# Banded attention of a trunk kernel: context scores as two fp32r passes of split operands, and both mask products at an item's end

## The chip, the cores and the metric

One core of one Trainium2 chip runs the whole step in one launch. The metric is the device time of a run in microseconds. The kernel before was run three times: 2095.13, 2097.68 and 2099.02 us, median 2097.68. All times of engines and instructions come from one further, profiled execution.

## The reference

One inference step of a backbone of two layers (width 1024) for 128 context tokens and 256 latent tokens that share all weights. Each layer is a half-step SwiGLU, a mixer stage and another half-step SwiGLU. The mixer stage projects the tokens with one matrix `w_in` into the columns of four branches (A long convolution, B differential attention, C windowed attention, D retention) and their gates, and adds their gated outputs up. The change lies in branch C, which has 8 query heads in 2 key heads of 64, and, for latent tokens, a band of keys plus all context keys in one softmax with a learned sink:

```python
    s_band = jnp.einsum('bnqhgd,bnkhd->bnhgqk', qb, kb).astype(jnp.float32) * scale
    s_band = jnp.where(valid[None, :, None, None], s_band, NEG_INF)
    s_ctx = jnp.einsum('bnqhgd,bchd->bnhgqc', qb, k_ctx).astype(jnp.float32) * scale
    s_sink = jnp.broadcast_to(sink.astype(jnp.float32).reshape(WIN_KV_HEADS, WIN_GROUP)[None, None, :, :, None, None],
...
    p = jax.nn.softmax(jnp.concatenate([s_band, s_ctx, s_sink], axis=-1), axis=-1)
```

Context tokens attend to the 128 context keys alone, in `window_dense_block`, with the same scale and sink. `NEG_INF` stands at band positions farther than 128 tokens.

## The kernel before, in words

All large products are made of two fp32r halves of each operand: a value is split into a high part and the rest (`split`, line 456: a copy on ScalarE, L412, rounds to the high part, a subtraction on VectorE, L389, makes the low part), and `mm3` (L383) adds high by high, low by high and high by low. The tokens stand as 384 columns, so most matmuls of TensorE (`mm`, L376) are 128x384: some 10,800 of them, called the main stream here, go through the weights in a fixed order. `run_plan` (L461) loads each weight block raw by a DMA of SyncE's queue, `splits` makes its halves wh and wl in four slots ahead of their use, and every half has some 24 main matmuls in these stages.

The branches' own work is written as generators (`diff_side`, `hy_side`, `win_side`, `ret_side`), and `pump` (L602) fits their steps between the main matmuls. It goes by modelled clocks of the engines: every helper (`mm`, `act`, `tt`) adds a modelled cost, and a step is taken when the modelled VectorE and ScalarE are not too far behind TensorE, when two PSUM banks are free, and when its inputs are due. A step taken writes its instructions into each engine's queue there; every engine then works its queue in order. New work, or more or fewer free tiles, therefore shifts where later steps land. Tiles come from three sets: L (30 of 512 columns), M (26 of 384 columns, and L if none is free), and B, the 8 PSUM banks, each handed out longest-free first.

`win_side` (L1525) does branch C of one layer. It normalises the queries, transposes them by `feat_mm` (four banks, one for each pair of heads, 128 context and 256 latent columns), and brings them into SBUF: the latent columns are split, in two halves of 64 partitions (one for each head), so that high and low part of a head stand above each other on 128 partitions (`qT`); the 128 context columns are copied plainly to `qc`, in fp32. Then the keys: reciprocal roots, norm, rotation, transposes, the latent keys split into `kh` and `kl`, the context keys copied plainly to `kc`.

Then 12 items (pair of heads `pr` 0 to 3, query tile `qt` 0 to 2; `qt` 0 is the context tile) go through `softmax_pipe` (L1382), which in its step i does `s3` of item i−4 (the product with the values), `s2` of i−3 (transposes), `s1` of i (scores), `s1c` of i−2 and `s1b` of i−1 (maximum, exponential, sums). `s1` fills two banks, one for each head c of the pair. A context item has one fp32 product of 64 partitions for each bank, which the trace shows as two records. A latent item has two fp32r products of 128 partitions and 384 columns (the stacked queries against `kh` and `kl`), then a product of the identity `identb` with the mask `maskb`, both bf16, 128x128, added to it. `s3` of a pair's last tile splits the pair's output from its bank into two M tiles, which frees that bank, and in the same step `s1` of the next pair but one's context item takes banks. When the branch is done, its output waits for the branch's weights in the main stream.

Of the kernel before, what the change touches and what calls it, by code (L numbers as in the profile page):

```python
# [11 lines left out]
F32R = mybir.dt.float32r  # L12
# [300 lines left out]
class Kern:  # L313
# [1211 lines left out]
    def win_side(self, l):  # L1525
        L, M, B, nc, S = self.L, self.M, self.B, self.nc, self.S
        while "wq" not in S:
            yield "w"
        ck, cv = L.get(), M.get()
# [5 lines left out]
        for t in range(3):  # L1535
            self.qk_norm(qs[t], 8, rs[:, 8 * t:8 * t + 8], t, self.sm(l, "gwq"), tl, 0)
            yield 0.0 if t < 2 else list(qs)
        qT, qc = [], L.get()
        for h in range(4):
            b = self.feat_mm(qs, 128 * h)  # L1540
            d = L.get(F32R)
            for c in range(2):
                r, o, n = slice(64 * c, 64 * c + 64), slice(64 - 64 * c, 128 - 64 * c), slice(256 * c, 256 * c + 256)
                self.split(d[r, n], d[o, n], b[r, 128:384])
            self.act(qc[:, 128 * h:128 * h + 128], b[:, 0:128])
            B.put(b)
            qT.append(d)
            if h % 2:
                yield 0.0
# [3 lines left out]
        kv = S.pop("wkv")  # L1553
# [11 lines left out]
        nc.gpsimd.dma_start(self.O["o_wk"][l], kv[0][:, 0:128])  # L1565
        nc.gpsimd.dma_start(self.O["o_wv"][l], kv[0][:, 128:256])
        L.put(tl)
        kT, kc = [], M.get()
        for h in range(2):
            b = self.feat_mm(kd + [ck], 128 * h)  # L1570
            kh, kl = M.get(F32R), M.get(F32R)
            self.split(self.nv(kh[:, :T]), self.nv(kl[:, :T]), self.pv(b[:, 128:512]))
            self.act(kc[:, 128 * h:128 * h + 128], b[:, 0:128])
            B.put(b)
            kT.append((kh, kl))
        L.put(ck, *kd)
        V = [k[:, 128:256] for k in kv] + [cv[:, 0:128]]
        yield qT + [qc, kc] + [x for p in kT for x in p]
        items = [(pr, qt) for pr in range(4) for qt in range(3)]
        py = {}  # L1580
        out = []
# [1 line left out]
        def s1(pr, qt):  # L1583
            nk = 384 if qt else 128
            kv_ = pr // 2
            ps = []
            for c in range(2):
                b = B.get()
                r = slice(64 * c, 64 * c + 64)
                if qt == 0:  # L1590
                    self.mm(b[:, :128], qc[r, 128 * pr:128 * pr + 128], kc[r, 128 * kv_:128 * kv_ + 128], True, True)
                else:
                    o = 256 * c + 128 * (qt - 1)
                    for i in range(2):
                        self.mm(b[:, :nk], qT[pr][:, o:o + 128], self.mv(kT[kv_][i][:, :nk]), i == 0, False)
                    mo = 128 if qt == 1 else 0
                    self.mm(b[:, mo:mo + 128], self.identb, self.maskb[:, 128 * (qt - 1):128 * qt], False, True)
                ps.append(b)
            return ps, nk, pr

        def s1b(ps, nk, pr):
# [37 lines left out]
        def s3(pr, qt, at):  # L1639
# [9 lines left out]
            if qt == 2:  # L1649
# [4 lines left out]
                out.append((hi, lo))  # L1654

        yield from self.softmax_pipe(items, s1, s1b, s1c, s1d, s2, s3)
        M.put(cv, kc, *[x for p in kT for x in p])
        L.put(qc, *qT, *kv)
        self.br[2] = out

    def ret_prep(self, l):
# [450 lines left out]
```

## Time and profile before

| what | value |
|---|---|
| time of the runs (median of three) | 2097.68 us |
| profiled execution, its own time | 2092.43 us |
| span in the profile | 2090.7 us |
| mean granted clock of TensorE | 0.996 |
| TensorE busy | 2060.9 us (99%) |
| VectorE busy | 1476.3 us (71%) |
| ScalarE busy | 960.1 us (46%) |
| share of the chain that ended last | TensorE 78%, VectorE 12%, ScalarE 4% |

The profiled execution's own time is 1.7 us over its span. TensorE's records overlap: a 128x384 matmul is recorded with some 0.33 us, while one starts about every 0.16 us, so its cost in a row of matmuls is the distance of starts and not the recorded length. A number in square brackets behind a row is the engine's idle time before it and what ended it. Names of tiles stand without their numbers: wh and wl are weight halves, hh and hl activations, raw the loaded weights, B a PSUM bank, L and M tiles, sm small columns.

### The profile page before, as it was taken

The page shows a single profiled execution, that of the slowest core. Times are in us where ns is not written, and L with a number is a line of the kernel's source. Part 1 is how long each engine was busy: PE and PEld are TensorE (multiplying, and loading weights), DVE is VectorE, ACT ScalarE, POOL GpSimd, SP SyncE. Part 2 cuts the span into 40 slices and gives each one's busy share as a digit, 9 for nine tenths or more (in the row PEclk, how much of TensorE's full clock was granted, in tenths as well). Part 3 has the DMA queues.
Part 4 walks back from the last instruction along what each step waited for, and adds up shares of the span by engine and source line. Part 5 has one row for each costly group of instructions (what it writes and reads, how often), then busy time and mean ns, then how long its engine had stood idle before and what let it go on. Part 6 is the DMA issues. An engine that isn't in the chain of part 4 may idle for free.

```text
span 2090.7 us, 33262 instructions
## 1 busy us (share of the span) xinstructions
PE 2060.9 (99%) x12994; PEld 1958.0 (94%) x12994; DVE 1476.3 (71%) x3156; ACT 960.1 (46%) x1661; POOL 31.4 (2%) x62
## 2 busy tenths in 40 slices
PE   9999999999999999999999999999999999999999
PEld 7999988899988998999999999888999889899999
DVE  5789779578764788877578995686787656754443
ACT  4443446664455435334444333456535543443332
POOL 0000000000000000000000000000000000000000
PEclk9999999999999999999999999999999999999999
DMA  8658463323232536662366773632233223533432
GB/s 317 241 201 321 151 226 124 113 102 122 113 116 99 194 139 233 222 210 102 109 244 229 246 255 120 248 133 104 101 130 124 102 101 108 198 121 115 156 120 100
DMA packets 88206, 340.39 MB, mean 163 GB/s; under 512 B 10416, under 2 KB 12912, under 8 KB 64624
## 3 DMA queue, kind: packets, MB, share of 16 engines
q1 hardware_dynamic: 83952, 326.41, 44.1%
q0 software_dynamic: 3808, 11.71, 1.7%
q8 instruction: 102, 1.67, 0.3%
q14 instruction: 56, 0.46, 0.1%
q10 hardware_dynamic: 288, 0.14, 0.0%
HBM read 334.82 MB, written 3.41 MB: 162 GB/s over the span
## 4 chain that ended last, share of the span: by engine, by line
PE 78%; DVE 12%; ACT 4%; issue 3%; DMA 3%; SPq 0%; ACTq 0%; DVEq 0%
PE B L376 76%; DVE L L400 3%; DVE wl L389 3%; ACT wh L412 2%; DMA L<-in_ada 2%; PE B L418 2%; DVE M L389 1%; DVE L L389 1%; DVE M L400 1%; ACT L L412 1%; ACT M L412 1%; DVE x L400 1%; DMA raw<-in_w1a 0%; DMA L<-in_adap 0%; SPq L582 0%
## 5 line engine op out<-in xcount | busy, mean ns | idle before, releaser
L389 DVE TENSOR_TENSOR wl<-raw,wh 128x1024 fp32r<-128x1024 f32 (+1 forms) x500 | 563.3, 1138 | 294.2 <-ACT wh L412 290.9
L376 PE MATMUL B<-hh,wh 128*128 128x384 f32 x2176 | 719.7, 331 | 2.0 <-ACT hh L412 2.0
L376 PE MATMUL B<-hh,wl 128*128 128x384 f32 x2176 | 711.7, 327 | 4.0 <-DVE wl L389 4.0
L376 PE MATMUL B<-hl,wh 128*128 128x384 f32 x2176 | 711.3, 327 | 0.8 <-DVE hl L400 0.8
L412 ACT ACTIVATE wh<-raw 128x1024 fp32r<-128x1024 f32 (+1 forms) x500 | 483.1, 982 | 326.3 <-PE B L376 250.7
L376 PE MATMUL B<-M,wh 128*128 128x384 f32 x1816 | 456.8, 328 | 0.2 <-ACT M L412 0.2
L376 PEld LDWEIGHTS B<-hh,wh 128*128 128x128 f32 x2176 | 412.2, 189 | 16.1 <-issue 9.3
L376 PEld LDWEIGHTS B<-hh,wl 128*128 128x128 f32 x2176 | 412.3, 189 | 6.7 <-DVE wl L389 6.2
L376 PEld LDWEIGHTS B<-hl,wh 128*128 128x128 f32 x2176 | 412.3, 189 | 1.9 <-DVE hl L400 1.9
L376 PEld LDWEIGHTS B<-M,wh 128*128 128x128 f32 x1816 | 321.3, 189 | 3.9 <-issue 1.4
L376 PE MATMUL B<-M,wl 128*128 128x384 f32 x928 | 303.1, 327 | 0.0
L400 DVE SCALAR_TENSOR_TENSOR L<-L,L 128x512 f32<-128x512 f32 x320 | 202.7, 691 | 2.2 <-ACT L L412 1.7
L412 ACT ACTIVATE M<-B 128x384 f32<-128x384 f32 (+2 forms) x254 | 113.9, 465 | 162.7 <-PE B L376 125.1
L376 PEld LDWEIGHTS B<-M,wl 128*128 128x128 f32 x928 | 175.7, 189 | 0.6 <-DVE wl L389 0.2
L389 DVE TENSOR_TENSOR M<-M,M 128x384 f32<-128x384 f32 (+2 forms) x200 | 110.1, 556 | 82.8 <-ACT M L412 80.5
L412 ACT ACTIVATE M<-M 128x384 fp32r<-128x384 f32 (+2 forms) x108 | 53.2, 499 | 246.6 <-DVE M L389 228.6
L376 PE MATMUL B<-wh,hh 128*128 128x512 f32 (+1 forms) x336 | 124.5, 370 | 0.2 <-ACT hh L412 0.2
L376 PE MATMUL B<-wh,hl 128*128 128x512 f32 (+1 forms) x336 | 122.7, 365 | 0.6 <-DVE hl L400 0.6
L376 PE MATMUL B<-wl,hh 128*128 128x512 f32 (+1 forms) x336 | 122.5, 365 | 0.0
L412 ACT ACTIVATE L<-B 128x512 f32<-128x512 f32 (+7 forms) x186 | 88.0, 517 | 63.8 <-PE B L376 43.8
L389 DVE TENSOR_TENSOR M<-M,B 128x384 f32<-128x384 f32 x88 | 48.6, 552 | 61.3 <-ACT M L412 61.3
L400 DVE SCALAR_TENSOR_TENSOR x<-B,mod,x 128x128 f32<-128x128 f32 (+1 forms) x160 | 59.0, 414 | 25.0 <-PE B L376 24.3
(162 smaller groups left out, 1862.4 us busy)
## 6 DMA issues: line engine op xcount, KB each, us to landing
raw<-in_win SPq DMA_DIRECT2D x74, 1024.0 KB, 4.8
L<-in_ada SPq DMA_DIRECT2D x192, 256.0 KB, 5.8
raw<-in_w1b SPq DMA_DIRECT2D x44, 1024.0 KB, 4.8
raw<-in_w1a SPq DMA_DIRECT2D x41, 1024.0 KB, 4.9
L<-in_adap SPq DMA_DIRECT2D x96, 256.0 KB, 7.4
raw<-in_w2a SPq DMA_DIRECT2D x32, 704.0 KB, 4.1
raw<-in_w2b SPq DMA_DIRECT2D x32, 704.0 KB, 4.0
raw<-in_wbr SPq DMA_DIRECT2D x16, 1024.0 KB, 4.8
```

Source lines behind the costliest of these rows:

```text
L376: self.nc.tensor.matmul(out, lhsT, rhs, start=start, stop=stop, **kw)
L389: self.nc.vector.tensor_tensor(out, a, b, op=op)
L400: self.nc.vector.scalar_tensor_tensor(out, a, s, b, op0=op0, op1=op1, accum_out=accum_out)
L412: self.nc.scalar.activation(out, a, f, **kw)
L418: self.nc.tensor.transpose(out, a, self.ident)
```

## The change

In each layer the context queries are split too: for each pair of heads two splits of 64 partitions by 128 columns follow the two of the latent columns, alternating with them, and fill two L tiles of fp32r (`qc`, a list now) in place of one plain copy into one L tile. The context keys are split into one L tile (`kc`: high parts in columns 0 to 255, low parts behind) in place of a plain copy into an M tile. The scores of a context item become two fp32r products of 128 partitions for each bank, against the high and the low keys. In all items both banks are taken at the start of `s1`, and in latent items the two mask products come behind all four score products. What is computed is the same.

```diff
--- before.py
+++ after.py
@@ -1535,14 +1535,17 @@
         for t in range(3):
             self.qk_norm(qs[t], 8, rs[:, 8 * t:8 * t + 8], t, self.sm(l, "gwq"), tl, 0)
             yield 0.0 if t < 2 else list(qs)
-        qT, qc = [], L.get()
+        qT, qc = [], []
         for h in range(4):
             b = self.feat_mm(qs, 128 * h)
             d = L.get(F32R)
+            if h % 2 == 0:
+                qc.append(L.get(F32R))
             for c in range(2):
                 r, o, n = slice(64 * c, 64 * c + 64), slice(64 - 64 * c, 128 - 64 * c), slice(256 * c, 256 * c + 256)
                 self.split(d[r, n], d[o, n], b[r, 128:384])
-            self.act(qc[:, 128 * h:128 * h + 128], b[:, 0:128])
+                n = slice(256 * (h % 2) + 128 * c, 256 * (h % 2) + 128 * c + 128)
+                self.split(qc[-1][r, n], qc[-1][o, n], b[r, 0:128])
             B.put(b)
             qT.append(d)
             if h % 2:
@@ -1565,17 +1568,17 @@
         nc.gpsimd.dma_start(self.O["o_wk"][l], kv[0][:, 0:128])
         nc.gpsimd.dma_start(self.O["o_wv"][l], kv[0][:, 128:256])
         L.put(tl)
-        kT, kc = [], M.get()
+        kT, kc = [], L.get(F32R)
         for h in range(2):
             b = self.feat_mm(kd + [ck], 128 * h)
             kh, kl = M.get(F32R), M.get(F32R)
             self.split(self.nv(kh[:, :T]), self.nv(kl[:, :T]), self.pv(b[:, 128:512]))
-            self.act(kc[:, 128 * h:128 * h + 128], b[:, 0:128])
+            self.split(kc[:, 128 * h:128 * h + 128], kc[:, 256 + 128 * h:384 + 128 * h], b[:, 0:128])
             B.put(b)
             kT.append((kh, kl))
         L.put(ck, *kd)
         V = [k[:, 128:256] for k in kv] + [cv[:, 0:128]]
-        yield qT + [qc, kc] + [x for p in kT for x in p]
+        yield qT + qc + [kc] + [x for p in kT for x in p]
         items = [(pr, qt) for pr in range(4) for qt in range(3)]
         py = {}
         out = []
@@ -1583,19 +1586,19 @@
         def s1(pr, qt):
             nk = 384 if qt else 128
             kv_ = pr // 2
-            ps = []
-            for c in range(2):
-                b = B.get()
-                r = slice(64 * c, 64 * c + 64)
-                if qt == 0:
-                    self.mm(b[:, :128], qc[r, 128 * pr:128 * pr + 128], kc[r, 128 * kv_:128 * kv_ + 128], True, True)
-                else:
-                    o = 256 * c + 128 * (qt - 1)
-                    for i in range(2):
+            ps = [B.get(), B.get()]
+            for c, b in enumerate(ps):
+                for i in range(2):
+                    if qt == 0:
+                        o, k = 256 * (pr % 2) + 128 * c, 256 * i + 128 * kv_
+                        self.mm(b[:, :128], qc[pr // 2][:, o:o + 128], kc[:, k:k + 128], i == 0, i == 1)
+                    else:
+                        o = 256 * c + 128 * (qt - 1)
                         self.mm(b[:, :nk], qT[pr][:, o:o + 128], self.mv(kT[kv_][i][:, :nk]), i == 0, False)
-                    mo = 128 if qt == 1 else 0
+            if qt:
+                mo = 128 if qt == 1 else 0
+                for b in ps:
                     self.mm(b[:, mo:mo + 128], self.identb, self.maskb[:, 128 * (qt - 1):128 * qt], False, True)
-                ps.append(b)
             return ps, nk, pr
 
         def s1b(ps, nk, pr):
@@ -1654,8 +1657,8 @@
                 out.append((hi, lo))
 
         yield from self.softmax_pipe(items, s1, s1b, s1c, s1d, s2, s3)
-        M.put(cv, kc, *[x for p in kT for x in p])
-        L.put(qc, *qT, *kv)
+        M.put(cv, *[x for p in kT for x in p])
+        L.put(kc, *qc, *qT, *kv)
         self.br[2] = out
 
     def ret_prep(self, l):
```

The order of the instructions moves at three places that matter here. The first is ScalarE's queue at the query split of layer 0: B0 and B5 are the banks of the first two pairs of heads, L14 and L17 before (L0 and L17 now) their latent tiles `qT`, and L0 before (L14 now) the context tile `qc`. Before:

```order
L412 ACTIVATE L14_221_5347<-B0_180_5343 64x256 x2
L412 ACTIVATE L0_220_5342<-B0_180_5343 128x128
L412 ACTIVATE L17_222_5357<-B5_181_5353 64x256 x2
L412 ACTIVATE L0_220_5342<-B5_181_5353 128x128
L412 ACTIVATE L19_223_5373<-B1_182_5369 64x256 x2
```

Now:

```order
L412 ACTIVATE L0_220_5346<-B0_180_5342 64x256
L412 ACTIVATE L14_221_5347<-B0_180_5342 64x128
L412 ACTIVATE L0_220_5346<-B0_180_5342 64x256
L412 ACTIVATE L14_221_5347<-B0_180_5342 64x128
L412 ACTIVATE L17_222_5360<-B5_181_5356 64x256
L412 ACTIVATE L14_221_5347<-B5_181_5356 64x128
L412 ACTIVATE L17_222_5360<-B5_181_5356 64x256
L412 ACTIVATE L14_221_5347<-B5_181_5356 64x128
```

Each pair's copy of 128x128 has become two of 64x128, one behind each 64x256. In both orders a copy of the same bank waits for the subtraction that VectorE has just before it, and the first copy of the next pair waits for the transposes into its new bank alone.

The second is TensorE's queue in layer 0 at the context item of head pair 2 (the two rows into B3 and B6 before, into B2 and B0 now), behind the value products of a pair's last tile and two transposes; wh138 to wh140 are halves of weights in the main stream, L20, L26 and M20 the values, L22 (L16 now) the context keys `kc`, L0 (L2 now) the context queries `qc`. Before:

```order
L376 MATMUL B0_244_6588<-hl013_3446,wh138_6340 128x384
L376 MATMUL B6_232_6468<-M10_258_6554,L20_209_4531 64x128
L376 MATMUL B6_232_6468<-M19_259_6560,L20_209_4531 64x128
L376 MATMUL B6_232_6468<-M10_258_6554,L26_211_4536 64x128
L376 MATMUL B6_232_6468<-M19_259_6560,L26_211_4536 64x128
L376 MATMUL B6_232_6468<-M10_258_6554,M20_200_5143 64x128
L376 MATMUL B6_232_6468<-M19_259_6560,M20_200_5143 64x128
L418 MATMUL B7_245_6627<-const_78,M5_256_6502 128x128
L418 MATMUL B5_246_6631<-const_78,M11_257_6503 128x128
L376 MATMUL B3_247_6635<-L22_241_6240,L0_220_5342 128x128
L376 MATMUL B6_248_6637<-L22_241_6240,L0_220_5342 128x128
L376 MATMUL B4_243_6587<-hh014_3439,wh139_6399 128x384
```

Now:

```order
L376 MATMUL B4_246_6671<-hl011_3444,wh140_6452 128x384
L376 MATMUL B0_236_6543<-M6_257_6615,L20_209_4531 64x128
L376 MATMUL B0_236_6543<-M23_258_6621,L20_209_4531 64x128
L376 MATMUL B0_236_6543<-M6_257_6615,L26_211_4536 64x128
L376 MATMUL B0_236_6543<-M23_258_6621,L26_211_4536 64x128
L376 MATMUL B0_236_6543<-M6_257_6615,M20_200_5143 64x128
L376 MATMUL B0_236_6543<-M23_258_6621,M20_200_5143 64x128
L418 MATMUL B5_247_6694<-const_78,M16_255_6577 128x128
L418 MATMUL B7_248_6698<-const_78,M2_256_6578 128x128
L376 MATMUL B2_249_6702<-L16_252_6253,L2_224_5380 128x128 x2
L376 MATMUL B0_250_6703<-L16_252_6253,L2_224_5380 128x128 x2
L376 MATMUL B3_245_6670<-hh012_3437,wh140_6452 128x384
```

The item stood between the last matmul of wh138 and the first of wh139; it now stands within the half of wh140, 12 main matmuls behind that half's start. It comes 36 main matmuls later in the stream. In both orders its second bank is the one whose output the step has just handed to `split` (B6 before, B0 now). The same holds for the context item of pair 3, from behind 3048 main matmuls to behind 3084; the first context item stays in its place.

The third is TensorE's queue at the first latent item of layer 0 (banks B7 and B2 in both). Before:

```order
L376 MATMUL B7_220_6311<-L23_242_6246,L14_221_5347 128x384
L376 MATMUL B7_220_6311<-L16_243_6247,L14_221_5347 128x384
L376 LDWEIGHTS identb_104
L376 MATMUL B7_220_6311<-maskb_105,identb_104 128x128
L376 MATMUL B2_221_6315<-L23_242_6246,L14_221_5347 128x384
L376 MATMUL B2_221_6315<-L16_243_6247,L14_221_5347 128x384
L376 LDWEIGHTS identb_104
L376 MATMUL B2_221_6315<-maskb_105,identb_104 128x128
```

Now:

```order
L376 MATMUL B7_220_6328<-L4_241_6259,L0_220_5346 128x384
L376 MATMUL B7_220_6328<-L12_242_6260,L0_220_5346 128x384
L376 MATMUL B2_221_6329<-L4_241_6259,L0_220_5346 128x384
L376 MATMUL B2_221_6329<-L12_242_6260,L0_220_5346 128x384
L376 LDWEIGHTS identb_104
L376 MATMUL B7_220_6328<-maskb_105,identb_104 128x128
L376 LDWEIGHTS identb_104
L376 MATMUL B2_221_6329<-maskb_105,identb_104 128x128
```

The four score products stand together and the two mask products, each with its load of the identity, behind them. Between the first item and the end of branch C items of layer 0 come up to 42 main matmuls later and those of layer 1 up to 12 later or 6 earlier, the retention steps behind them follow, and the last items of layer 0 end some 18 to 30 main matmuls later; ahead of the first item of a layer TensorE's order is the same in both.

## Rows read from the trace of the kernel before

**Rows 1.** TensorE's waits of the whole span, by releaser: us in total, times, longest us
```profile
PE B L376 <- DVE M L389: 7.3, 7, 1.8
PE B L376 <- DVE wl L389: 6.0, 10, 1.5
```

**Rows 2.** Timeline of VectorE, layer 0's query split: start, us, instruction, idle before
```profile
495.88 0.42 DVE L389 TENSOR_TENSOR L<-B,L 64x256 fp32r<-64x256 f32 x1 [0.60 <-ACT L L412]
...
497.77 0.42 DVE L389 TENSOR_TENSOR L<-B,L 64x256 fp32r<-64x256 f32 x1 [0.60 <-ACT L L412]
```

**Rows 3.** Timeline of ScalarE, the same stretch
```profile
498.22 0.38 ACT L412 ACTIVATE L<-B 64x256 fp32r<-64x256 f32 x1 [0.48 <-DVE L L389]
...
500.99 0.28 ACT L412 ACTIVATE L<-B 128x128 f32<-128x128 f32 x1 [0.49 <-DVE L L389]
```

**Rows 4.** VectorE's groups by form: reading 128 columns of a bank
```profile
L404 DVE TENSOR_REDUCE sm<-B 128x1 f32<-128x128 f32 x32 | 7.7, 283 | 0.0
```

**Rows 5.** Timeline of VectorE, behind the query split of layer 0
```profile
503.39 0.17 DVE L396 TENSOR_SCALAR sm<-sm 128x6 f32<-128x6 f32 x1
...
508.11 3.21 DVE L400 SCALAR_TENSOR_TENSOR M<-M,smt,M 128x127 f32<-128x127 f32 x8 [1.70 <-ACT M L412]
...
511.84 2.35 DVE L389 TENSOR_TENSOR wl<-raw,wh 128x1024 fp32r<-128x1024 f32 x2
```

**Rows 6.** Timeline of TensorE, the same stretch
```profile
511.27 0.33 PE L376 MATMUL B<-hh,wh 128*128 128x384 f32 x1
513.11 0.43 PE L376 MATMUL B<-hh,wl 128*128 128x384 f32 x1 [1.52 <-DVE wl L389]
```

**Rows 7.** Timeline of VectorE, behind the query split of layer 1
```profile
1571.17 2.36 DVE L389 TENSOR_TENSOR wl<-raw,wh 128x1024 fp32r<-128x1024 f32 x2 [2.28 <-ACT wh L412]
...
1579.74 2.35 DVE L389 TENSOR_TENSOR wl<-raw,wh 128x1024 fp32r<-128x1024 f32 x2
```

**Rows 8.** Timeline of TensorE, where layer 1 wants those two wl
```profile
1573.30 0.33 PE L376 MATMUL B<-hh,wl 128*128 128x384 f32 x1
...
1581.13 0.38 PE L376 MATMUL B<-wl,hh 128*128 128x512 f32 x1
```

**Rows 9.** A window behind a wait: stretch, length, TensorE busy, granted clock, DMA
```profile
634.60:638.00 3.40, 3.40 (x15) 0.50 0.00 0
```

**Rows 10.** Timeline of TensorE, second halves of context items (pairs 2, 3; both layers)
```profile
617.43 0.48 PE L376 MATMUL B<-L,L 64*128 64x128 f32 x2 [1.29 <-DVE M L389]
...
633.45 0.48 PE L376 MATMUL B<-L,L 64*128 64x128 f32 x2 [1.29 <-DVE M L389]
...
1654.24 0.48 PE L376 MATMUL B<-M,L 64*128 64x128 f32 x2 [0.40 <-DVE M L389]
...
1671.86 0.48 PE L376 MATMUL B<-M,L 64*128 64x128 f32 x2 [0.46 <-DVE M L389]
```

**Rows 11.** Timeline of TensorE, the first context item
```profile
586.23 0.33 PE L376 MATMUL B<-L,wh 128*128 128x384 f32 x1
...
587.05 0.33 PE L376 MATMUL B<-M,wh 128*128 128x384 f32 x1
587.30 0.49 PE L376 MATMUL B<-L,L 64*128 64x128 f32 x4
587.72 0.43 PE L376 MATMUL B<-M,wh 128*128 128x384 f32 x1
587.99 0.33 PE L376 MATMUL B<-M,wl 128*128 128x384 f32 x1
```

**Rows 12.** Timeline of TensorE, transposes of 128x128
```profile
1617.92 1.04 PE L418 MATMUL B<-const,L 128*128 128x128 f32 x8
```

**Rows 13.** Timeline of TensorE, a masked item's second half and what follows
```profile
590.56 0.23 PE L376 MATMUL B<-maskb,identb 128*128 128x128 bf16 x1
590.60 0.41 PE L376 MATMUL B<-M,wh 128*128 128x384 f32 x1
590.84 0.33 PE L376 MATMUL B<-M,wl 128*128 128x384 f32 x1
```

## The prediction, as written before the changed kernel ran

> **What bounds the kernel now.** I read the page first, then the waits of TensorE, then the timelines of the places that the change touches. TensorE is busy 99% of the span (table above), and its waits are few: all those for VectorE's subtractions into M tiles make 7.3 us in 7 waits, those for the low weight halves wl 6.0 us in 10 [rows 1]. So one more microsecond of matmuls costs one microsecond, and ScalarE and VectorE matter only where TensorE stands and waits for them. There are few such places, and two lie right behind the code that changes: behind the split of the queries, and between the two halves of a context item. A change of 0.2% (4.2 us) is about what a measurement of this kernel can tell from none.
>
> **The query split, layer 0.** The four pairs of heads follow each other at 497.77 − 495.88 = 1.89 us: VectorE has a 64x256 subtraction of 0.42, behind 0.60 of idling for ScalarE [rows 2], and ScalarE idles 0.48 for VectorE, starting 0.03 after it ends (497.77 + 0.42 = 498.19; 498.22) [rows 2, 3]. It is one chain of copy, subtract, copy, subtract. The change adds a second ping-pong of this kind after each: of four new operations per pair of heads one copy takes the place of the old 128x128 copy and one subtraction lies beside the next pair's first copy, as the last piece of the order shown above lets it. What is left on the chain is one round trip: copy 0.28 as the 128x128 copy [rows 3], subtraction 0.28 as VectorE's reading of 128 PSUM columns [rows 4], and 0.03 behind each: 0.62. Four pairs: **+2.5 us**. If each cost no more than VectorE's smallest operations (0.17 at 503.39) [rows 5], it is 4 x 2 x 0.20 = 1.6; if as much as the 256-column subtraction, 4 x 2 x 0.45 = 3.6. Nothing excludes either end; the 128-column rows are nearest.
>
> Does it reach TensorE? The chain goes on without a gap: wh and wl of the next half, the reciprocal root of the keys (503.39 on), norm, convolution (508.11, 3.21 us), the next wl at 511.84 [rows 5]. TensorE stands for that wl from 511.27 to 513.11, which is 1.84 against a normal spacing of 0.16 [rows 6]: it already waits at the end of this chain, so all of the 2.5 us arrives there. ScalarE's and VectorE's order between the split and this wl doesn't change.
>
> **The query split, layer 1.** The same chain, except that the roots follow the last subtraction at once, so the last pair's second round trip counts too: five trips, 3.1 us. The wl at 1571.17 (two in 2.36, so 1.18 each) would come at 1574.3 and be done at 1575.5; TensorE wants it at 1573.30: 2.2 us. The second wl, now at 1579.74, would be done at 1579.74 + 3.1 + 1.2 = 1584.0; TensorE wants it at 1581.13 [rows 7, 8]: 2.9 us in all, the first wait within it. There was no stall here: **+2.9 us** (with the ends above, five trips of 0.40 or 0.90: 1.8 to 4.3).
>
> **TensorE's clock behind a stall.** From 634.60 to 638.00 the granted clock is 0.50, its lower level of 1.2 GHz [rows 9]; before, TensorE had stood over 1 us for a bank (633.45) [rows 10]. It costs half of 3.4, 1.7 us. The stall of 1.7 us at 511 brought no fall [rows 6], so a stall alone does not decide it. I take the number of falls as unchanged: that one goes with its stall (below), and one comes behind one of the new stalls, which are longer. **0**, ends −1.7 and +3.4.
>
> **Context scores.** From 587.05, the last ordinary matmul before an item, to 587.99, the second after it, are 0.94 us; two ordinary spacings of 0.164 (586.23 to 587.05 in five) leave 0.61 for the item, whose two half-array products run side by side, in two records each [rows 11]. Four full-array passes take their place. No row shows an fp32r pass over 128 columns; 128x128 transposes follow at (1.04 − 0.27)/7 = 0.11 [rows 12], so 0.44: −0.17 for an item, 8 items, **−1.4 us**. Ends: as short as half a transpose's, 0.22, −3.1; as long as one of the two fp32 passes from 587.30 to 587.72, 0.21 each, 0.84: +1.8 [rows 11].
> The Trainium skill, page "TensorEngine Tiling (Array Packing)", section "Overview", speaks against this edit: with a contraction of 64 or less, two row tiles give up to twice the speed, and the change gives them up. The trace agrees that the old pair runs abreast [rows 11]; by the rule alone the term would be the upper end, +1.8 for −1.4, and the sum +4.8.
>
> **The mask products.** A mask and an ordinary matmul take 590.84 − 590.56 = 0.28, so a mask costs 0.12, part of it the exposed start of its successor (0.41 against 0.33) [rows 13]. Two together have one exposed change of operand fewer. I take 0.04 saved for each of 16 items, **−0.7 us**; ends 0 and a whole mask, −1.9.
>
> **The bank waits.** In the context items of head pairs 2 and 3 the second half's bank is the one that the finished output just before is copied out of; TensorE waits 1.29 twice in layer 0 and 0.40 and 0.46 in layer 1 [rows 10]. In layer 0 the item stands right where a weight half ends, and ScalarE and VectorE have the next wh and wl ahead of the copies (the wl of 1.2 us). The planner, whose modelled clocks change by the new work, now puts these items 12 matmuls behind such a place (second and third pieces of the order). The waits stay, but I take layer 1's length: 2 x 0.86, **−1.7 us**; ends −2.6 (no wait) and 0. Other items get new neighbours; new waits of that size may arise, ±1.
>
> **Hidden.** The key split: two more subtractions and copies where VectorE idles and the copies wait for VectorE anyway: 0; uncovered, two trips a layer, 2.5. SP's loads and POOL's retention loads change places by some rows; no DMA is late in a touched stretch: 0. Up to the first item TensorE's order is the same.
>
> Sum: +2.5 + 2.9 + 0 − 1.4 − 0.7 − 1.7 = **+1.6 us**. The profiled execution took 2092.4, so this one would take 2094.0; it lies 5.3 below the median of the runs shown, 2097.7, from which I forecast **2099.3 us**.
>
> **Rivals.** *The clock decides (slower).* Both new stalls are followed by 3.4 us at the lower clock and the old fall stays: 1.6 + 2 x 1.7 (one was netted against the old) = +5.0, 2102.7. For it: the new stall at 511 is 4.2 us, over twice any before; against it: none fell at 511 now. It decides from two falls more than now. Chance 0.2.
> *Four passes are dear (slower).* The context term takes its upper end, +1.8: sum +4.8, 2102.5. For it: no fp32r row is that short; against it: the transposes at 0.11 [rows 12]. Chance 0.07. It is what the rule of the Trainium skill's page "TensorEngine Tiling (Array Packing)", named above, would give.
> *The splits hide (faster).* If the new operations overlap the old ones, both chain terms fall and no new stall comes, while the old fall goes: −1.4 − 0.7 − 1.7 − 1.7 = −5.5, 2092.2. For it: source and target tiles of the new split differ from those beside it; against it: the order of waits keeps one PSUM bank's readers in turn. Chance 0.15.
> *No bank gain.* The context items wait as before: +3.3, 2101.0, still within the bound. Chance 0.13, beside 0.45 for the forecast.
>
> **Numbers.** Faster by over 0.2%: 0.17 (the splits hide, with a little from mis-sized waits). Slower: 0.27 (the first two rivals, whose lower part stays within the bound, and the forecast's upper tail). Within: 0.56. The range goes from the faster rival to the clock's, with 1 to 2 us for the spread of the runs (2095.1 to 2099.0): 2091 to 2105.
>
> **What would show it.** Right: a wait for wl near 511 of about 4 us, two new waits for wl near 1573 and 1581, pairs of heads at 2.5 us instead of 1.9, waits of about half a microsecond in the context items of layer 0, context passes 0.11 apart. Wrong: no stall at 1573, or pairs of heads still at 1.9 (the splits hide), or a stretch of 0.50 clock behind each new stall.

## The result, and the profile after

The changed kernel takes 2104.88 us (median of six runs, 2102.13 to 2107.81); the kernel before, with three runs more on the same chip, 2094.40 (2092.26 to 2099.02). The ratio is 1.0051, with a 95% interval of 1.0039 to 1.0063: **slower by 10.5 us**, where 1.6 were forecast. The chance given to slower was 0.27. (A ratio is taken over all runs and need not be the quotient of the two medians.)

Where did the time go? The main stream has the same 10,800 matmuls in both traces, so the start of the same matmul in both shows by how much the changed kernel lags, and the growth of the lag between two of them what a stage cost. Both profiled executions, worked out from the starts in the two traces:

| stretch (main matmuls) | lag grows by, us | forecast |
|---|---|---|
| up to the query split of layer 0 (2400) | +0.2 | 0 |
| query chain, layer 0 (to 2720) | +6.1 | +2.5 |
| branch C's items, layer 0 (2880 to 3310) | −3.1 | −1.7 −1.05 |
| retention tail and out-projection, layer 0 (to 3720) | +3.5 | 0 |
| norm behind it (to 3900) | +2.8 | 0 |
| query chain, layer 1 (8000 to 8160) | +3.6 | +2.9 |
| branch C's items, layer 1 (to 8600) | −1.2 | −1.05 |
| norm behind layer 1's mixer (to 9400) | +1.3 | 0 |

The rows add up to 13.2 us, the difference of the two profiled executions (2105.59 and 2092.43); the medians differ by less, because the execution profiled before was one of the faster ones.

First the chain. VectorE's timeline of the changed kernel at the query split of layer 0, against [rows 2] (a row with x2 holds the next pair's first operation too):

```profile
495.65 0.42 DVE L389 TENSOR_TENSOR L<-B,L 64x256 fp32r<-64x256 f32 x1 [0.45 <-ACT L L412]
496.42 0.82 DVE L389 TENSOR_TENSOR L<-B,L 64x128 fp32r<-64x128 f32 x2 [0.34 <-ACT L L412]
497.57 0.28 DVE L389 TENSOR_TENSOR L<-B,L 64x128 fp32r<-64x128 f32 x1 [0.34 <-ACT L L412]
498.31 0.42 DVE L389 TENSOR_TENSOR L<-B,L 64x256 fp32r<-64x256 f32 x1 [0.45 <-ACT L L412]
```

ScalarE's in the same stretch, against [rows 3]:

```profile
497.27 0.27 ACT L412 ACTIVATE L<-B 64x128 fp32r<-64x128 f32 x1 [0.48 <-DVE L L389]
497.89 0.38 ACT L412 ACTIVATE L<-B 64x256 fp32r<-64x256 f32 x1 [0.35 <-DVE L L389]
498.76 0.67 ACT L412 ACTIVATE L<-B 64x128 fp32r<-64x128 f32 x2 [0.49 <-DVE L L389]
```

From one pair's second 64x256 subtraction to the next pair's are 498.31 − 495.65 = 2.66 us where they were 1.89: 0.77 for the added round trip and not 0.62. The trip's own parts are as priced (subtraction 0.28, copy 0.27). The rest is in ScalarE's last row: the two instructions in it take 0.67, of which the second is a copy of 0.38, so the next pair's copy starts 0.3 us behind the small one. Before, ScalarE put two copies closer together; this row of the kernel before has 0.54 for a 128x128 copy (0.28) and a 64x256 copy (0.38):

```profile
499.10 0.54 ACT L412 ACTIVATE L<-B 128x128 f32<-128x128 f32 x2 [0.49 <-DVE L L389]
```

So some 0.13 of overlap in each pair is lost. Why the new small copy lets its successor in later, no run here shows.

TensorE in the same stretch, against [rows 6]:

```profile
511.30 0.33 PE L376 MATMUL B<-hl,wh 128*128 128x384 f32 x1
513.56 0.43 PE L376 MATMUL B<-hh,wh 128*128 128x384 f32 x1 [1.94 <-ACT wh L412]
516.48 0.69 PE L376 MATMUL B<-hh,wl 128*128 128x384 f32 x1 [2.49 <-DVE wl L389]
516.96 0.52 PE L376 MATMUL B<-hl,wh 128*128 128x384 f32 x1
517.28 0.52 PE L376 MATMUL B<-hh,wh 128*128 128x384 f32 x1
```

Four windows of the changed kernel (stretch, length, TensorE busy, granted clock, DMA):

```profile
515.50:522.40 6.90, 5.92 (x18) 0.51 0.69 258
774.90:781.90 7.00, 6.06 (x18) 0.51 0.42 150
805.60:812.60 7.00, 6.64 (x48) 0.51 0.25 81
1836.50:1840.00 3.50, 3.50 (x33) 0.51 0.00 0
```

It waits 1.94 for wh and then 2.49 for wl, 4.4 together, where it waited 1.52 in all. And then it runs at half speed: the matmuls that follow start 0.32 apart, and for 6.9 us the granted clock is 0.51, the level of 1.2 GHz (such a stretch is called a fall here). This alone costs 2.9 us (the lag grows from 3.4 at the first of them to 6.3). The three other windows are falls of the same kind: behind the out-projection's wait, in the norm behind it, and in layer 1's norm. The kernel before had two in its middle, near 634 [rows 9] and 771, each of 3.4 us; the mean granted clock of the whole span went from 0.996 to 0.992. In the middle of the span that makes some 23.8 us at the lower level (three times 6.8 and 3.4) where it was 6.8. By the lag, the fall behind the stall costs 2.9 and those in the two norms 2.8 and 1.3, and the one at 634, which is gone, gives 1.7 back. So some 5 of the 13.2 us are falls, and 8.5 at most, half of the added time at the lower level.

In layer 1 TensorE waits at the two places foreseen, against [rows 8], 1.55, 0.83 and 0.46:

```profile
1584.23 0.43 PE L376 MATMUL B<-hh,wh 128*128 128x384 f32 x1 [1.55 <-ACT wh L412]
1585.49 0.43 PE L376 MATMUL B<-hh,wl 128*128 128x384 f32 x1 [0.83 <-DVE wl L389]
...
1594.05 0.48 PE L376 MATMUL B<-wl,hh 128*128 128x512 f32 x1 [0.46 <-DVE wl L389]
```

### The profile page after: what moved, and what is told of

It is laid out like the page before. It is cut to its first block, busy times and chain, and to the rows that moved or that the text cites. A ratio compares the mean times of both kernels' runs of the same rounds, so it can differ in the third digit from the quotient of the medians.

```text
span 2103.8 us, 33298 instructions
## 1 busy us (share of the span) xinstructions
PE 2067.6 (98%) x12994; PEld 1963.2 (93%) x12994; DVE 1481.8 (70%) x3176; ACT 962.8 (46%) x1669; POOL 31.4 (1%) x62
## 4 chain that ended last, share of the span: by engine, by line
PE 79%; DVE 11%; ACT 4%; issue 3%; DMA 2%; SPq 0%; DVEq 0%; ACTq 0%
PE B L376 78%; DVE wl L389 3%; DVE L L400 2%; DVE L L389 2%; ACT wh L412 2%; PE B L418 2%; DMA L<-in_ada 1%; DVE M L389 1%; DVE M L400 1%; ACT L L412 1%; DMA raw<-in_w1a 1%; ACT M L412 1%; DVE x L400 0%; SPq L582 0%; DVE sm L389 0%
## 5 line engine op out<-in xcount | busy, mean ns | idle before, releaser
L412 ACT ACTIVATE L<-B 128x512 f32<-128x512 f32 (+8 forms) x195 | 90.8, 505 | 68.7 <-PE B L376 41.3
```

The costliest lines, as they stand in the source:

```text
L412: self.nc.scalar.activation(out, a, f, **kw)
```

## The experiments

Two theories. **A:** the longer query chain is the loss, by its stalls and by the clock that falls behind them. **B:** the moved order is the loss: the retention tail comes late (TensorE waits at 737 in the changed kernel), modulation work of VectorE falls between the steps of the out-projection at 768, and the falls near 775 and 806 stand behind these. The first runs set the chain (long or short) against the order (old or new); the change itself is the long chain with the new order, the kernel before the short chain with the old. Each run is compared with runs of the kernel before on its own chip: median 2093.60 for the first four, 2094.22 for the next three, 2093.68 for the last two.

**Long chain, old order.** `op` does nothing while `mute` is set, and the old cost is charged instead:

```diff
+                self.mute = True
                 self.split(qc[-1][r, n], qc[-1][o, n], b[r, 0:128])
+                self.mute = False
+            self.op("act", 0.094 + 128 / 1200, [qc[-1]], [b])
...
+                        self.mute = True
                         self.mm(b[:, :128], qc[pr // 2][:, o:o + 128], kc[:, k:k + 128], i == 0, i == 1)
+                        self.mute = False
+                        if i:
+                            self.op("pe", 4 * 128 / 2400, [b], [qc[pr // 2], kc])
```

(The key split likewise.)

> The change's instructions all stay, but the planner is charged the old costs for them, so that in layer 0 every other step stands where it stood before (in layer 1 some steps behind branch C's last items move by 6 to 12 main matmuls). Theory A (the longer query chain, and the clock behind its stall): pairs of heads at 2.5 us, a stall of 4.5 to 5 us near 511 with a stretch of 0.50 clock behind it, two waits of 2.8 us together near 1573, nothing new at 737 or 768: 7 to 9 us over the kernel before. Theory B (most of the loss is the moved order: the late retention tail at 737, the modulation work at 768, and the clock falls behind them): the chain's plain 2.5 and 2.9 us stay, the rest goes, 2 to 5 us over the kernel before.

Measured: 2106.28, ratio 1.0048 (1.0034 to 1.0062); that is 10 us by the ratio and 12.7 by the medians, over the 7 to 9 that theory A was given and far over theory B's. The windows of its profile have the clock fall behind the stall, and this time also behind layer 1's:

```profile
516.70:523.70 7.00, 5.72 (x18) 0.51 0.65 246
1585.10:1588.60 3.50, 3.50 (x14) 0.51 0.78 286
```

Theory B falls as the explanation of the loss: with the old order the loss is the same.

**Short chain, new order.** The context columns are copied plainly into `qf`, as before, and split from there in the keys' stage:

```diff
-                n = slice(256 * (h % 2) + 128 * c, 256 * (h % 2) + 128 * c + 128)
-                self.split(qc[-1][r, n], qc[-1][o, n], b[r, 0:128])
+            self.act(qf[:, 128 * h:128 * h + 128], b[:, 0:128])
...
+            if t == 1:
+                qc = [L.get(F32R), L.get(F32R)]
+                for c in range(2):
+                    r, o = slice(64 * c, 64 * c + 64), slice(64 - 64 * c, 128 - 64 * c)
+                    self.split(qc[c][r, :512], qc[c][o, :512], qf[r, :512])
+                L.put(qf)
```

> The context queries are copied plainly in the query stage, as before, and split later from SBUF, within the keys' stage, in two splits of 64x512; everything else as in the change, with the planner's true costs, so that from the third item on the order is that of the change. Theory A: pairs of heads at 1.89 us, 1.7 us of stall near 511 and none near 1573, no clock fall behind either: 3 us under to 1 us over the kernel before. Theory B: the late tail at 737 and the modulation work at 768 stay and cost 4 us, with clock falls behind them up to 8: 3 to 7 us over the kernel before.

Measured: 2095.47, ratio 1.0011 (0.9998 to 1.0024): most of the loss is gone with the chain. What is left, some 2 us, lies between the two theories' ranges. TensorE's timeline at 512 is the old one again, with the old wait, and no fall stands behind it. At the out-projection, its second row here, it still waits 3.13:

```profile
512.04 0.43 PE L376 MATMUL B<-hh,wl 128*128 128x384 f32 x1 [1.53 <-DVE wl L389]
...
768.48 0.43 PE L376 MATMUL B<-mh,wh 128*128 128x384 f32 x1 [3.13 <-ACT wh L412]
```

The kernel with the long chain and the old order waits 1.15 there (its lines are numbered four higher, by the inserted ones):

```profile
777.61 0.43 PE L380 MATMUL B<-mh,wh 128*128 128x384 f32 x1 [1.15 <-ACT wh L416]
```

So the late out-projection belongs to the order, and the loss to the chain.

**Short chain, old order**, both edits together.

> Both: the context queries are split later as in the run before, and the planner is charged the old costs, so that in layer 0 the order is the old one. What is left is the cheaper context scores and mask products. Both theories: 1 to 3 us under the kernel before (context 1.4, masks 0.7). If it is not under the kernel before, the gains that I priced on TensorE aren't there.

Measured: 2096.41, ratio 1.0001 (0.9991 to 1.0011). By the ratios the old order is worth 2 us against the new one, by the medians the new one is 0.9 better: the two can't be told apart. The gains on TensorE, priced at 2.1, are not in the time, a miss. The trace shows where they go. The first context item is 0.17 shorter, as in the change, but where TensorE waits in a later latent item for VectorE or ScalarE, it now waits longer. In layer 1, the kernel before and then this one:

```profile
1641.22 0.43 PE L376 MATMUL B<-M,L 128*128 128x384 f32 x1 [0.83 <-DVE L L400]
...
1658.77 0.59 PE L376 MATMUL B<-L,L 128*128 128x384 f32 x2 [0.33 <-ACT M L412]
```

```profile
1643.34 0.59 PE L380 MATMUL B<-M,L 128*128 128x384 f32 x2 [1.10 <-DVE L L404]
...
1660.88 0.59 PE L380 MATMUL B<-L,L 128*128 128x384 f32 x2 [0.59 <-ACT M L416]
```

In layer 1 nothing of the gain is left in the lag, in layer 0 some 0.5 (table below, less the fall at 634).

**The masks alone**, on the kernel before:

```diff
+            ps = [B.get(), B.get()]
...
-                    self.mm(b[:, mo:mo + 128], self.identb, self.maskb[:, 128 * (qt - 1):128 * qt], False, True)
-                ps.append(b)
+            if qt:
+                mo = 128 if qt == 1 else 0
+                for b in ps:
+                    self.mm(b[:, mo:mo + 128], self.identb, self.maskb[:, 128 * (qt - 1):128 * qt], False, True)
```

> The kernel before with one part of the change, both banks at the item's start and both mask products at its end. Layer 0's order stays; in layer 1 some steps behind branch C's last items move by 6 to 12 main matmuls. Both theories: 0 to 2 us under the kernel before, 0.7 by my price. If the second half of an item waits for its bank before the first mask could have hidden it, 1 us over.

Measured: 2096.56, ratio 1.0007 (0.9996 to 1.0017). No gain.

**The scores alone**, the change without its mask part:

```diff
-            if qt:
-                mo = 128 if qt == 1 else 0
-                for b in ps:
-                    self.mm(b[:, mo:mo + 128], self.identb, self.maskb[:, 128 * (qt - 1):128 * qt], False, True)
+                if qt:
+                    self.mm(b[:, mo:mo + 128], self.identb, self.maskb[:, 128 * (qt - 1):128 * qt], False, True)
```

> The change without its mask part: the masks stay behind each half's two products, as before; splits and context scores as in the change. The long chain stays, so 10 us over the kernel before as the change; over the change by what the masks save, 0.7 us by my price, 1.1 by the starts of the first masked item in the change's trace.

Measured: 2104.31, ratio 1.0048 (1.0035 to 1.0060); against the change's 1.0051, from another chip, the mask part makes no difference that these runs can tell.

**Half the chain, old order.** The first two pairs as in the change, the others later:

```diff
+                if h < 2:
+                    n = slice(256 * h + 128 * c, 256 * h + 128 * c + 128)
...
+                    self.split(qc[0][r, n], qc[0][o, n], b[r, 0:128])
```

> As the run with the short chain and the old order, but the context queries of the first two pairs of heads are split at once, as in the change, and only those of the other two later. Two round trips of 0.76 us in place of four: a stall of 1.7 + 1.5 = 3.2 us near 511 in layer 0, and 1.3 us of new waits near 1573 in layer 1. If the loss is the trips' length alone, it is half of that of the long chain with the old order, in stalls about 3 us, less the 1 us of cheaper matmuls: 2 us over the kernel before. If the clock decides by the length of the stall, a stretch at 0.50 either stands behind the stall (then 4 to 6 us over) or not (then 1 to 2 us over).

Measured: 2101.63, ratio 1.0037 (1.0025 to 1.0050), 7.4 us over the kernel before and not 2; with no fall behind the stall, 1 to 2 were expected. TensorE's wait at the stall is 2.48 us, behind one of 0.31, and the window behind it has the full clock:

```profile
518.80 0.43 PE L380 MATMUL B<-hh,wl 128*128 128x384 f32 x1 [2.48 <-DVE wl L393]
```

```profile
518.00:525.00 7.00, 6.20 (x40) 1.00 0.73 280
```

The stalls are near the size expected: in its trace the lag grows by 1.6 us in layer 0's query chain and by 2.6 in layer 1's, of which 1.3 stand in the short chain with the old order too and come from the later split. The rest of its lag came elsewhere: 4.1 us before the query split and 2.7 in layer 1's norm, and its trace has the clock at 0.50 for 6.8 us from 309 and again from 1831, in norms, where the program does the same as before. This is no accident of one execution: all five runs had a mean granted clock of 0.993 or 0.994, where the nine of the kernel before had 0.994 to 0.997. So the expectation missed: half the chain is not half the loss, and more than half of its trace's lag comes from falls away from the stall. Why this kernel meets more of those is open.

**The change with its stalls filled.** If TensorE's standing brings the clock down, work in the wait should keep it up. Main matmuls are counted in `mm`:

```diff
+            n = {2545: 44, 8089: 16}.get(self.mains, 0)
...
+            self.nc.tensor.matmul(b[:, :256], self.identb, self.maskb, start=True, stop=True)
```

> The change with 44 matmuls of the identity with the mask (bf16, 256 columns, result unused) put ahead of main matmul 2545, and 16 ahead of 8089, where TensorE waits for the split behind the query chain; the planner doesn't see them. The waits stay as long as they are, but TensorE works in them. If the clock falls behind the long stall because TensorE stood, the 6.8 us at 0.50 near 516 are gone and 2.9 us with them: 2.5 to 3 us under the change. If that stretch has another cause, it stays, and the time is that of the change.

Measured: 2102.01, ratio 1.0041 (1.0028 to 1.0055). That is 2.9 us under the change's median, which is from another chip, and 2.3 under the scores alone on the same one. The intervals overlap, so the times alone don't settle it, but the profile is plain. TensorE's timeline (L378 is the fill, L392 the line of `mm` in this file):

```profile
510.31 0.33 PE L392 MATMUL B<-hl,wh 128*128 128x384 f32 x1
510.47 4.98 PE L378 MATMUL B<-maskb,identb 128*128 128x256 bf16 x44
515.21 0.41 PE L392 MATMUL B<-hh,wh 128*128 128x384 f32 x1
515.49 0.43 PE L392 MATMUL B<-hh,wl 128*128 128x384 f32 x1
```

And windows over the fill and behind it:

```profile
507.00:513.00 6.00, 6.00 (x47) 1.00 0.02 4
513.00:520.00 7.00, 7.00 (x52) 1.00 0.48 169
```

The stop is as long as before, 5.18 us from the last ordinary matmul to the one that wants wl (510.31 to 515.49; in the change 511.30 to 516.48), but the clock stays at 1.00, and the chain costs this trace 3.2 us in place of 6.1. **The fall behind the stall comes from TensorE's standing.** Theory A holds for the stall and for the fall behind it; the falls in the norms are still there in this run.

The lag's growth in the profiled executions, stage by stage as above:

| run | before 2400 | chain, layer 0 | items, layer 0 | to 3720 | norm, to 3900 | chain, layer 1 | items, layer 1 | norm, to 9400 |
|---|---|---|---|---|---|---|---|---|
| the change | +0.2 | +6.1 | −3.1 | +3.5 | +2.8 | +3.6 | −1.2 | +1.3 |
| scores alone | −0.8 | +6.3 | −3.3 | +3.7 | +2.8 | +3.7 | −1.5 | +1.5 |
| change, filled | −0.8 | +3.2 | −3.0 | +3.3 | +2.8 | +3.6 | −1.2 | +1.4 |
| long chain, old order | +1.7 | +5.9 | +1.0 | +0.1 | 0.0 | +4.6 | 0.0 | +1.4 |
| half chain, old order | +4.1 | +1.6 | −0.5 | +0.1 | 0.0 | +2.6 | 0.0 | +2.7 |
| short chain, new order | −1.1 | 0.0 | −2.4 | +3.1 | +0.9 | +1.3 | −1.1 | +1.3 |
| short chain, old order | +3.0 | 0.0 | −2.2 | 0.0 | 0.0 | +1.3 | 0.0 | +1.4 |
| masks alone | +0.3 | 0.0 | +1.6 | +0.1 | +1.1 | 0.0 | +0.2 | +2.5 |

The chain's columns follow the chain, and the column to 3720 follows the order, in every row. In the norms and in the stretch before 2400 the program is the same, and what differs is falls. Before 2400 they follow neither. The norm to 3900 has +2.8 in all three kernels with both the long chain and the new order, and 0 to 1.1 in the others; why is open. In layer 1's norm all eight kernels of the table have a fall, and the one profile of the kernel before has none, so this column may say more about that one profile than about them.

**The fills without the change.** The last two runs put such fills into the known waits of the kernel before (edit below), and of the short chain with the old order (the same, with 12 or 6 in the context items).

```diff
+            n = {2546: 14, 3673: 10, 3674: 8}.get(self.mains, 0)
...
+        n = {2: 14, 3: 17, 4: 4, 5: 4, 6: 17}.get(self.norms, 0)
...
+                    if c and pr > 1:
+                        self.fill(11 if l == 0 else 4)
```

> The kernel before with unused matmuls of the identity with the mask (bf16, 256 columns) put into TensorE's longest waits: 14 ahead of main matmul 2546, 10 and 8 at the change of weights in the out-projection near 768, 14, 17, 4, 4 and 17 in the norms between the stages, 11 and 4 between the halves of the context items of pairs 2 and 3. The waits stay as long as they are, or grow by what a fill is too long. If a clock fall comes only where TensorE stood, the stretches at 0.50 near 634, 771 and in the norms go, 1.7 us each: 2 to 5 us under the kernel before. If falls come by chance anywhere: the same time.

> The run with the short chain and the old order (context scores in four fp32r passes, masks at the end, context queries split later) with the same fills, 12 between the halves of the context items of pairs 2 and 3 (6 in one of layer 1). If the falls come from TensorE's standing: 2 to 5 us under the kernel before, as the filled kernel before, and if the cheaper scores and masks count when no falls blur them, 1 to 2.5 us under that one. If they don't count: the time of the filled kernel before.

Measured: the filled kernel before 2091.82 (2090.76 to 2093.17), ratio 0.9988 (0.9980 to 0.9997); the filled short chain 2092.16 (2090.78 to 2094.61), ratio 0.9985 (0.9976 to 0.9995). Both are under the kernel before, by 2.5 and 3.1 us after the ratios and by 1.9 and 1.5 after the medians, and some 13 under the changed one (from another chip), and behind the start no fall is left (windows of the filled kernel before over the query chain, the out-projection and the two norms):

```profile
508.00:516.00 8.00, 8.00 (x54) 1.00 0.23 86
764.00:777.00 13.00, 11.59 (x69) 1.00 0.31 102
795.00:806.00 11.00, 10.10 (x107) 1.00 0.53 192
1818.00:1830.00 12.00, 11.10 (x116) 1.00 0.50 175
```

The runs of the kernel before on that chip went from 2091.87 to 2099.55, 7.7 us; the filled ones spread over 2.4 and 3.8. Among the 21 runs of the kernel before, the 13 with a mean granted clock of 0.995 to 0.997 took 2091.87 to 2094.96, and the eight with 0.992 or 0.993 took 2097.02 to 2099.55. The gain looks like the slow part of that spread, cut off. Between the two filled kernels there is still no difference: the 1 to 2.5 us of cheaper scores and masks don't show, a miss. Against the filled kernel before, the trace of the filled short chain gains 0.8 in layer 0's items and nothing in layer 1's, and gives back 1.3 by the later split in layer 1.

## Why the prediction was wrong

The mechanism of the main term was right, and with it the two places: TensorE stood at the end of the query chain in both layers, and all that the chain grew by arrived there. The steps that failed:

- **"I take the number of falls as unchanged ... 0."** This is the step that made a small loss a large one. The fall behind the new stall in layer 0 stands in all three profiles with a long chain and unfilled wait, lasts twice as long as the one that I had priced at 1.7, and costs 2.9; with the other falls, the time at the lower clock grew by some 17 us. The rival in which the clock decides had the mechanism and the place, and pointed to a stall over twice any before; with 4.4 us against 1.8 it was that. Its price of +5.0 was still half of the loss: it took falls of 3.4 us, and none behind the out-projection or in the norms.
- **"copy 0.28 ..., subtraction 0.28 ..., and 0.03 behind each: 0.62."** The trip is 0.77. Four of them made 3.2 and not 2.5, five in layer 1 3.6 and not 2.9. The sum of an operation's lengths was right; what it overlapped with before was not counted.
- **"The waits stay, but I take layer 1's length ... −1.7."** The context items' waits in layer 0 did fall, from 1.29 [rows 10] to 0.64, but a new one of 0.59 stands five microseconds behind each, in the next latent item (TensorE's timeline of the changed kernel):

```profile
627.62 0.44 PE L376 MATMUL B<-L,L 128*128 128x128 f32 x2 [0.64 <-DVE M L389]
...
632.15 0.59 PE L376 MATMUL B<-L,L 128*128 128x384 f32 x2 [0.59 <-ACT M L412]
```

  The new wait belongs to the order: in layer 0 it stands in the scores alone too, which has the masks as before, and in no run with the old order, where the old waits stand. The items' gain of 3.1 in layer 0 is in good part the fall at 634, which is gone (1.7); that the column comes near the −2.75 of the forecast is luck. That the fall goes with its stall is not shown either: the short chain with the old order waits 1.53 and 1.52 at these places and the clock stays at 1.00, while the masks alone and the long chain with the old order have a fall behind each of these two waits.
- **"SP's loads and POOL's retention loads change places ...: 0."** I looked at the queues that load and not at what VectorE does later. The order that moved by up to 42 main matmuls delayed the retention tail and put modulation work between two steps of the out-projection. TensorE's timeline of the changed kernel at both places:

```profile
739.00 0.33 PE L418 MATMUL B<-const,L 128*128 128x128 f32 x1 [1.00 <-DVE L L389]
...
775.26 0.69 PE L376 MATMUL B<-mh,wh 128*128 128x384 f32 x1 [3.13 <-ACT wh L412]
```

  And VectorE's ahead of the second, where the operations on 512 and 8 columns are the modulation work:

```profile
766.85 1.23 DVE L389 TENSOR_TENSOR wl<-raw,wh 128x1024 fp32r<-128x1024 f32 x1 [0.31 <-ACT wh L412]
...
768.60 0.69 DVE L400 SCALAR_TENSOR_TENSOR L<-L,L 128x512 f32<-128x512 f32 x1
...
769.42 0.17 DVE L389 TENSOR_TENSOR mod<-M,gb 128x8 f32<-128x8 f32 x1
...
770.18 0.55 DVE L400 SCALAR_TENSOR_TENSOR M<-M,B 128x384 f32<-128x384 f32 x1
```

  It costs 3 us in each run with the new order and nothing in each with the old. In the time of the runs the two orders can't be told apart (short chain, above); branch C's items in layer 1 gain 1.2 by the same order.
- **Context scores and masks** were priced well for one item and still moved nothing. The first context item of the changed kernel and a masked item:

```profile
593.31 0.33 PE L376 MATMUL B<-M,wh 128*128 128x384 f32 x1
593.47 0.56 PE L376 MATMUL B<-L,L 128*128 128x128 f32 x4
593.87 0.38 PE L376 MATMUL B<-M,wh 128*128 128x384 f32 x1
594.08 0.33 PE L376 MATMUL B<-M,wl 128*128 128x384 f32 x1
...
595.71 0.33 PE L376 MATMUL B<-M,wh 128*128 128x384 f32 x1
595.87 0.81 PE L376 MATMUL B<-L,L 128*128 128x384 f32 x4
596.52 0.29 PE L376 MATMUL B<-maskb,identb 128*128 128x128 bf16 x2
596.62 0.41 PE L376 MATMUL B<-M,wh 128*128 128x384 f32 x1
596.86 0.33 PE L376 MATMUL B<-M,wl 128*128 128x384 f32 x1
```

  From 593.31 to 594.08 are 0.77 against 0.94 before [rows 11]: −0.17 as forecast. The masked item takes from 595.71 to 596.86, 1.15; before, the same stretch went from this row to 590.84 [rows 13], 1.22:

```profile
589.62 0.33 PE L376 MATMUL B<-M,wh 128*128 128x384 f32 x1
```

  Over both layers this would be 2 us. The step that failed is to count each item's gain as the span's: with the old order the waits of 0.83 and 0.33 in layer 1 grow to 1.10 and 0.59, as shown above, and of the 1.05 forecast for each layer 0.5 is left in layer 0 and nothing in layer 1. (With the new order layer 1's items gain 1.2, but there the waits have moved as well.) The Trainium skill's rule on row tiles (page "TensorEngine Tiling (Array Packing)", section "Overview") would have made the item dearer. It did not get dearer in the trace: four full-array passes take 593.87 − 593.47 = 0.40, and the pair abreast took 0.42. But the data type changed along with the tile, so this is no test of the rule itself.

The base was 3.3 us off as well: 2097.7 was the median of three runs, and 2094.4 is that of six; the difference of 10.5 doesn't hang on it. It is luck of this base that 2104.88 lies inside the stated range of 2091 to 2105: the range ends 7.3 us above its base, and the loss was 10.5.

## What to carry to other kernels

Work added to a chain that another engine already waits for costs its whole round trips, and the overlaps that they break, so look first for a place where the same work stands off that chain: here the same splits, done later from SBUF, cost 1.3 us of lag (all in layer 1) in place of 9.7. Price a stall on TensorE twice, as its length and as the clock that may fall behind it. A gain on TensorE can be real at its own place and be lost a few lines on, where the engine then waits longer for another; follow it through the next wait before you count it. Filling the waits makes the runs steadier, so that smaller differences can be seen.

## What the runs showed that was not expected

- The clock's falls explain most of the spread between runs of one kernel: with the waits filled it fell from 7.7 us to 2.4 (3.8 in the other filled kernel), and the mean granted clock of the profile rose from 0.996 to 0.998.
- Unused matmuls made a kernel faster, by 0.12%, with no work saved.
- Not settled: how often each kernel meets a fall in its norms, and what decides, besides the wait, whether one comes. A wait of 1.5 us at 511 had none behind it in four profiles, one of 2.5 had none in one, 4.4 in two steps had one in three of three.
